# A single-core decoder trunk: the scale row as a one-row product, its load first, filled weight buffers, and a new step list for the pooling mixer

## The chip, the cores and the metric

The kernel runs on 1 core of one Trainium2 chip. The metric is device time in microseconds (us) of one execution. The kernel before takes 899.64 us, the median of 3 runs (898.89 to 899.78 us).

## The reference

The reference is a small transformer trunk over 512 tokens of 1024 channels with two layers. Layer 0 mixes tokens by causal pooling, layer 1 by stick-breaking attention, and each is followed by a squared-ReLU MLP with sandwich RMSNorm. The change touches only the pooling mixer of layer 0:

```
h = rms_norm(x, mix_pre_g[0])
for g, w in enumerate((2, 4, 8, 16)):        # four groups of 256 channels
    y[:, g] = mean of the last w tokens of h[:, g]  -  h[:, g]
    m[:, g] = y[:, g] @ pool_w[g]            # 256 x 256
m = m * pool_scale                           # one factor per channel
x = x + rms_norm(m, mix_post_g[0])
h = rms_norm(x, mlp_pre_g[0])
x = x + rms_norm(square(relu(h @ w_up[0])) @ w_down[0], mlp_post_g[0])
```

## The kernel before

**Tiles.** Tokens lie in four tiles of 128 (`x0` to `x3`, 128 x 1024 fp32, 512 KB each). A fp32 product with one half as two rounded parts (`xnh`, `xnl` against high and low weights) makes the big products of the MLP; the mixer's own products are plain fp32, which TensorE does in two passes each.

**The mixer's stages.** For each token tile: the sum of squares (`q`, halves on ScalarE and VectorE for tiles 0 and 1, whole on ScalarE for 2 and 3), the reciprocal root on GpSimd (`v`), the pooling bands scaled by it (`b`, tile `own`), the pooling as a product of `x` with `own` (`p`, TensorE, line 875), its copy from PSUM to SBUF (`c`, ScalarE), the part that reaches over from the tile before (`f`, VectorE, line 892), the 256 x 256 maps (`m`, TensorE, line 903), squares (`s`, ScalarE, line 316) and product with the post gain (`g`, VectorE, line 368) of the result, its reciprocal root (`V`), the sum into `x` (`a`, VectorE, line 387), squares of `x` (`S`), root (`W`), norm (`n`, line 430), transposes (`t`, TensorE, line 438), and the split of the transposed tile into high (`h`, ScalarE, line 448) and low (`l`, VectorE, line 457). The digits behind a letter are the token tile and the half. Four up products of the MLP follow inside the mixer (`u`, lines 764 to 768; 24 products of 256 columns each, over token tiles 0 and 1); `i` and `k` split their weights (lines 920 and 924).

**The scale.** `pool_scale` and the pre gain are multiplied into the pooling weights (`w`, VectorE, line 832, four pieces of 256 columns for each half). The weights lie channel by partition, so the scale row is spread over 128 partitions by a product with a tile of ones (`r`, line 821): `row` is a 128 x 1024 tile whose first partition holds the row and whose others are filled with zeros on VectorE and GpSimd; `e` copies the result from PSUM.

**What sets the order.** `MIX_ORDER` is the list of these steps. Inside it the program order of TensorE, ScalarE, VectorE and GpSimd is exactly that list, so a step that waits holds every later step of its engine. `z8` is eight products on a zero tile, ahead of everything else on TensorE. SyncE's queue issues the loads in the order in which they are written, and a load that must wait for a buffer holds all loads behind it. The scale row alone is loaded from ScalarE's queue, after the table load of line 134 and both fills.

Of the kernel before, what the change touches and what calls it, by code (L numbers as in the profile page):

```python
# [10 lines left out]
F32 = mybir.dt.float32  # L11
# [4 lines left out]
P = 128  # L16
D = 1024
# [16 lines left out]
NS = [slice(0, 512), slice(512, 1024)]  # L34
# [10 lines left out]
def woven(x, c, n=S):  # L45
# [13 lines left out]

MIX_ORDER = [  # L60
    (w[0], [int(w[1:])] if w[0] == "z" else [int(c) for c in w[1:]])
    for w in """z8 q00 q01 r1 v0 b0 q10 r0 q11 v1 p02 p01 b1 p00 c02 e0 p12 c01 p11 w0 e1 p10 c00 c12 q2 q3 m00 w1 c11 v2 c10
    s00 f11 m01 m11 s01 b2 j0 v3 f10 m10 p22 g00 b3 i0 s11 p20 V0 g01 p21 p32 s10 a01 a00 V1 k0 S00 g10 S01 g11
    p31 c20 c21 p30 c31 c22 a11 f20 a10 W0 m20 n01 n00 S11 f21 g20 S10 t01 c30 c32 f30 W1 s20 t00 n10 f31 h00
    m21 t10 n11 i1 l00 t11 h10 k1 m31 s21 h01 l10 g21 V2 l01 i2 a20 m30 a21 s31 h11 s30 S20 l11 g31 S21 u0 V3 W2
    u1 g30 a31 a30 n21 i3 S31 n20 t21 t20 S30 k2 k3 h20 W3 h21 n30 u2 n31 t30 l20 t31 l21 u3 h30 h31 l30 l31""".split()
]


# [49 lines left out]
R_SCALE, R_MIX_POST0, R_MLP_PRE0, R_MLP_POST0, R_MIX_POST1, R_MLP_POST1 = range(6)  # L119
# [5 lines left out]
def trunk(ctx, tc, x, bands, grow, pw, wup, wdn, wq, wk, wv, wo, out):  # L125
    nc = tc.nc
# [4 lines left out]
    psum = pool("psum", 8, space=bass.MemoryType.PSUM)  # L131
    dram = pool("dram", space=bass.MemoryType.DRAM)

    nc.scalar.preload_act_table_set("sigmoid_and_others")

    uid = [0]

# [24 lines left out]
    def spare_tile():  # L162
        return work.tile([P, D], F32, tag="spare", name=name("spare"))
# [3 lines left out]
    def gain_row(r, t=None):  # L167
        t = work.tile([P, D], F32, tag="grow", name=name("grow")) if t is None else t
        rows.append(nc.sync.dma_start(t, grow[r : r + 1, :].broadcast_to((P, D))))
        return t  # L170
# [603 lines left out]


    with tc.tile_pool(name="mix0", bufs=1, reuse_waits="tile") as mp:
        warm = mp.tile([P, 512], mybir.dt.bfloat16, tag="warm", name="warm")
        nc.gpsimd.memset(warm, 0.0)

# [5 lines left out]
        later = packed[:, :half].bitcast(mybir.dt.bfloat16).rearrange("p (w c) -> p w c", w=NW)  # L785
        first = packed[:, half:].rearrange("p (w c) -> p w c", w=NW)

        row = mp.tile([P, D], F32, tag="row", name="row")
        nc.vector.memset(row[:, NS[0]], 0.0)
        nc.gpsimd.memset(row[:, NS[1]], 0.0)  # L790
        ones = mp.tile([P, P], F32, tag="ones", name="ones")
        nc.gpsimd.memset(ones, 1.0)
        at = D + P + 4 * KC
        wpool = [mp.tile([P, n], F32, tag=f"pw{i}", name=f"pw{i}") for i, n in enumerate((at, D))]
        nc.scalar.dma_start(row[:1], grow[R_SCALE : R_SCALE + 1, :])
        with tc.manual_schedule(engines={mybir.EngineType.SP}):
            nc.sync.dma_start(packed, bands)
            nc.sync.dma_start(xt[1], x[TS[1], :])
            nc.sync.dma_start(wpool[0], pw[:, :at])
            nc.sync.dma_start(xt[2], x[TS[2], :])  # L800
            nc.sync.dma_start(wpool[1], pw[:, at:])
            nc.sync.dma_start(xt[3], x[TS[3], :])
            gpost = gain_row(R_MIX_POST0)
            gpre0 = gain_row(R_MLP_PRE0, spare_tile())
# [613 lines left out]
```

## Time and profile before

| What | us |
|---|---|
| median of 3 runs | 899.64 |
| lowest and highest run | 898.89, 899.78 |
| the profiled execution | 899.84 |
| its span in the profile | 898.1 |
| TensorE (PE) busy | 888.9 (99%) |
| VectorE (DVE) busy | 690.4 (77%) |
| ScalarE (ACT) busy | 555.6 (62%) |
| GpSimd (POOL) busy | 37.8 (4%) |

The profiled execution lies 1.7 us above its span, which is what lies around the span, and 0.2 us above the median. Busy time of an engine is the time in which at least one of its instructions runs. PE's products overlap: one of 256 columns lasts 0.38 us in the records while the next one starts 0.216 us later, so a group's own length is its first start to the next group's first start. PEld is the weight load that goes ahead of a product; DMA landings count from the issue.

### The profile page before, as it was taken

How to read it: one execution, taken by the hardware profiler on the slowest of the kernel's cores; microseconds unless marked ns; L12 is line 12 of the kernel's file. 1: busy time of each engine (PE TensorE's matmuls, PEld its weight loads, DVE VectorE, ACT ScalarE, POOL GpSimd, SP SyncE). 2: the span in 40 equal slices, each digit the busy share in tenths (PEclk: the TensorE clock that was granted, in tenths of full speed). 3: DMA queues.
4: the chain of work that ended last, by engine and by line, in shares of the span. 5: the costliest groups of instructions: out<-in, count | busy, mean ns of one | idle time of the engine just before them, and what ended most of it. 6: DMA issues, size and time to landing. Idle time of an engine off the chain costs nothing.

```text
span 898.1 us, 12323 instructions
## 1 busy us (share of the span) xinstructions
PE 888.9 (99%) x4688; PEld 786.5 (88%) x4688; DVE 690.4 (77%) x800; ACT 555.6 (62%) x984; POOL 37.8 (4%) x78
## 2 busy tenths in 40 slices
PE   9999999999999999999999999999999999999997
PEld 6998888888888888888999888998888888888886
DVE  6876799998988977268777478884696976968866
ACT  6667679898796947256455464875545444444632
POOL 3200000000000004000000000200000000000002
PEclk9999999999999999999999999999999999999999
DMA  8446969889698750643152272442514233133002
GB/s 303 147 148 217 344 233 340 326 277 410 220 342 285 285 189 2 209 166 134 56 187 93 95 281 71 153 176 96 186 40 164 79 140 117 47 141 118 24 1 94
DMA packets 42685, 155.73 MB, mean 173 GB/s; under 512 B 4225, under 2 KB 4353, under 8 KB 42626
## 3 DMA queue, kind: packets, MB, share of 16 engines
q1 hardware_dynamic: 42624, 154.94, 47.9%
q8 instruction: 37, 0.61, 0.3%
q14 instruction: 22, 0.18, 0.1%
q10 hardware_dynamic: 2, 0.00, 0.0%
HBM read 121.38 MB, written 33.55 MB: 173 GB/s over the span
## 4 chain that ended last, share of the span: by engine, by line
PE 87%; DVE 4%; DMA 4%; ACT 3%; issue 2%; POOL 0%; SPq 0%; POOLq 0%; ACTq 0%; DVEq 0%
PE ps L638 24%; PE ps L767 14%; PE ps L764 14%; PE ps L768 14%; PE ps L331 4%; PE ps L333 4%; PE ps L332 4%; DMA xn<-in_wdn 2%; PE ps L1133 2%; PE ps L1114 2%; PE ps L1158 2%; PE ps L903 1%; PE ps L438 1%; DVE w L313 1%; DMA x<-in_x 1%
## 5 line engine op out<-in xcount | busy, mean ns | idle before, releaser
L638 PE MATMUL ps<-w,a 128*128 128x512 f32 x1176 | 266.3, 379 | 0.7 <-ACT a L312 0.7
L767 PE MATMUL ps<-xnh,w 128*128 128x512 f32 (+1 forms) x704 | 253.4, 362 | 0.0
L768 PE MATMUL ps<-xnl,w 128*128 128x512 f32 (+1 forms) x704 | 252.8, 360 | 0.0
L764 PE MATMUL ps<-xnh,w 128*128 128x512 f32 (+1 forms) x704 | 252.2, 360 | 0.3 <-DVE w L924 0.3
L638 PEld LDWEIGHTS ps<-w,a 128*128 128x128 f32 x1176 | 222.0, 189 | 32.9 <-ACT a L312 1.1
L764 PEld LDWEIGHTS ps<-xnh,w 128*128 128x128 f32 x704 | 132.9, 190 | 15.9 <-DVE w L924 0.4
L768 PEld LDWEIGHTS ps<-xnl,w 128*128 128x128 f32 x704 | 133.5, 190 | 15.2
L767 PEld LDWEIGHTS ps<-xnh,w 128*128 128x128 f32 x704 | 133.0, 190 | 15.3
L192 DVE TENSOR_TENSOR w<-raw,w 128x1024 fp32r<-128x1024 f32 x58 | 70.8, 1221 | 48.4 <-ACT w L190 48.4
L190 ACT CAST w<-raw 128x1024 fp32r<-128x1024 f32 x58 | 60.6, 1044 | 69.2 <-PE ps L764 68.2
L647 DVE TENSOR_TENSOR y<-ps,y 128x512 f32<-128x512 f32 x124 | 83.7, 684 | 24.5 <-PE ps L638 24.2
L312 ACT CAST a<-r 128x768 fp32r<-128x768 f32 (+1 forms) x60 | 47.4, 790 | 56.0 <-PE ps L638 36.5
L312 ACT CAST w<-e 128x1536 fp32r<-128x1536 f32 (+1 forms) x30 | 41.8, 1392 | 34.3 <-DVE e L612 26.2
L313 DVE TENSOR_TENSOR a<-r,a 128x768 fp32r<-128x768 f32 (+1 forms) x60 | 53.9, 898 | 8.3 <-ACT a L312 8.3
L1095 DVE TENSOR_TENSOR_SCAN e<-u,begin 128x1280 f32<-128x1280 f32 x16 | 45.2, 2825 | 18.6 <-ACT u L1079 17.9
L313 DVE TENSOR_TENSOR w<-e,w 128x1536 fp32r<-128x1536 f32 (+1 forms) x30 | 49.3, 1644 | 0.7 <-ACT w L312 0.5
L202 ACT ACTIVATE apart<-apart,eye 128x128 f32<-128x128 f32 (+1 forms) x128 | 42.4, 409 | 0.0
L313 DVE TENSOR_TENSOR w<-w,w 128x1536 fp32r<-128x1536 f32 (+1 forms) x20 | 33.0, 1648 | 4.7 <-ACT w L312 4.7
L674 ACT ACTIVATE r<-r 128x512 f32<-128x512 f32 x56 | 35.3, 630 | 1.3
L313 DVE TENSOR_TENSOR w<-xn,w 128x1536 fp32r<-128x1536 f32 (+1 forms) x20 | 33.0, 1649 | 3.7 <-ACT w L312 3.3
L673 ACT ACTIVATE r<-ps 128x512 f32<-128x512 f32 x56 | 33.1, 591 | 3.9 <-PE ps L764 3.9
L312 ACT CAST w<-w 128x1536 fp32r<-128x1536 f32 (+1 forms) x20 | 27.7, 1385 | 5.9 <-DMA w<-in_wdn 5.9
(148 smaller groups left out, 1293.4 us busy)
## 6 DMA issues: line engine op xcount, KB each, us to landing
raw<-in_wup SPq DMA_DIRECT2D x64, 512.0 KB, 3.8
w<-kept SPq DMA_DIRECT2D x60, 512.0 KB, 4.3
kept<-wx SPq DMA_DIRECT2D x30, 512.0 KB, 5.2
kept<-apart SPq DMA_DIRECT2D x24, 512.0 KB, 5.9
w<-in_wdn SPq DMA_DIRECT2D x8, 1536.0 KB, 7.4
xn<-in_wdn SPq DMA_DIRECT2D x8, 1536.0 KB, 8.3
apart<-in_wq SPq DMA_DIRECT2D x7, 512.0 KB, 6.9
kept<-spare SPq DMA_DIRECT2D x6, 512.0 KB, 6.0
```

Source lines behind the costliest of these rows:

```text
L190: nc.scalar.copy(hi, raw)
L192: nc.vector.tensor_tensor(out=lo, in0=raw, in1=hi.bitcast(F32), op=ALU.subtract)
L202: nc.scalar.mul(c, c, gc[:, at : at + 1])
L312: latest["act"] = nc.scalar.copy(hi, src)
L313: latest["dve"] = nc.vector.tensor_tensor(out=lo, in0=src, in1=hi.bitcast(F32), op=ALU.subtract)
L331: nc.tensor.matmul(dst, ah, bh, start=start, stop=False)
L638: nc.tensor.matmul(bank, a[:, x, q, TS[t]], woven(w[:, z, q], NS[0]), start=start and q == 0 and k == 0, stop=q == self.n - 1 and k == 2, ...
L647: nc.vector.tensor_tensor(out=part, in0=bank, in1=part, op=ALU.add)
L764: nc.tensor.matmul(pu[:, cols], wl[:, k, :], moving(xnh, k), start=False, stop=k == KC - 1)
L767: nc.tensor.matmul(pu[:, cols], wh[:, k, :], moving(xnh, k), start=k == 0, stop=False)
L768: nc.tensor.matmul(pu[:, cols], wh[:, k, :], moving(xnl, k), start=False, stop=False)
L1095: nc.vector.tensor_tensor_scan(out=self.e[:, ::-1], data0=self.u[:, 1:][:, ::-1], data1=begin[:, ::-1], initial=0.0, op0=ALU.mult, op1=ALU ...
```

## The change

The zero fills of `row` go, and `row` becomes a single partition; the product that spreads it has one row instead of 128. Its load is the first instruction of ScalarE, ahead of the activation table load. GpSimd fills the first 512 columns of the second weight tile and the 1184 columns of the first with zeros, and the loads of those tiles must wait for the fills. On SyncE's queue the second weight tile goes ahead of `x2`. The step list is written anew, with one zero product fewer.

```
--- before.py
+++ after.py
@@ -59,11 +59,12 @@
 
 MIX_ORDER = [
     (w[0], [int(w[1:])] if w[0] == "z" else [int(c) for c in w[1:]])
-    for w in """z8 q00 q01 r1 v0 b0 q10 r0 q11 v1 p02 p01 b1 p00 c02 e0 p12 c01 p11 w0 e1 p10 c00 c12 q2 q3 m00 w1 c11 v2 c10
-    s00 f11 m01 m11 s01 b2 j0 v3 f10 m10 p22 g00 b3 i0 s11 p20 V0 g01 p21 p32 s10 a01 a00 V1 k0 S00 g10 S01 g11
-    p31 c20 c21 p30 c31 c22 a11 f20 a10 W0 m20 n01 n00 S11 f21 g20 S10 t01 c30 c32 f30 W1 s20 t00 n10 f31 h00
-    m21 t10 n11 i1 l00 t11 h10 k1 m31 s21 h01 l10 g21 V2 l01 i2 a20 m30 a21 s31 h11 s30 S20 l11 g31 S21 u0 V3 W2
-    u1 g30 a31 a30 n21 i3 S31 n20 t21 t20 S30 k2 k3 h20 W3 h21 n30 u2 n31 t30 l20 t31 l21 u3 h30 h31 l30 l31""".split()
+    for w in """z7 q00 q01 r0 r1 v0 b0 q10 q11 v1 p00 p01 b1 p02 e0 c01 e1 c02 p12 w0 c00 c12 w1 p10 p11 c10 c11 m00 f11
+    m01 q2 v2 q3 m11 s00 f10 s01 m10 s11 b2 g00 i0 p21 g01 p20 v3 j0 V0 b3 s10 g11 a00 S00 a01 c21 c20 p22 p31
+    V1 S01 g10 p30 k0 c22 a10 f20 a11 c31 m20 p32 S10 W0 f21 S11 c30 W1 s20 c32 n01 n00 t01 i1 m21 g20 f30 s21
+    n10 t10 f31 t00 n11 t11 g21 k1 h00 V2 h10 h01 l00 a21 h11 a20 m30 l10 l11 l01 m31 u0 S21 S20 s31 W2 i2 s30
+    V3 n20 n21 t21 t20 g31 h20 g30 a31 h21 S31 a30 k2 u1 S30 i3 W3 l20 n30 u2 t30 n31 t31 h31 h30 k3 l21 l31
+    l30 u3""".split()
 ]
 
 
@@ -131,7 +132,6 @@
     psum = pool("psum", 8, space=bass.MemoryType.PSUM)
     dram = pool("dram", space=bass.MemoryType.DRAM)
 
-    nc.scalar.preload_act_table_set("sigmoid_and_others")
 
     uid = [0]
 
@@ -774,6 +774,10 @@
 
 
     with tc.tile_pool(name="mix0", bufs=1, reuse_waits="tile") as mp:
+        row = mp.tile([1, D], F32, tag="row", name="row")
+        with tc.manual_schedule(engines={mybir.EngineType.Activation}):
+            nc.scalar.dma_start(row, grow[R_SCALE : R_SCALE + 1, :])
+            nc.scalar.preload_act_table_set("sigmoid_and_others")
         warm = mp.tile([P, 512], mybir.dt.bfloat16, tag="warm", name="warm")
         nc.gpsimd.memset(warm, 0.0)
 
@@ -785,20 +789,18 @@
         later = packed[:, :half].bitcast(mybir.dt.bfloat16).rearrange("p (w c) -> p w c", w=NW)
         first = packed[:, half:].rearrange("p (w c) -> p w c", w=NW)
 
-        row = mp.tile([P, D], F32, tag="row", name="row")
-        nc.vector.memset(row[:, NS[0]], 0.0)
-        nc.gpsimd.memset(row[:, NS[1]], 0.0)
-        ones = mp.tile([P, P], F32, tag="ones", name="ones")
+        ones = mp.tile([1, P], F32, tag="ones", name="ones")
         nc.gpsimd.memset(ones, 1.0)
         at = D + P + 4 * KC
         wpool = [mp.tile([P, n], F32, tag=f"pw{i}", name=f"pw{i}") for i, n in enumerate((at, D))]
-        nc.scalar.dma_start(row[:1], grow[R_SCALE : R_SCALE + 1, :])
+        nc.gpsimd.memset(wpool[1][:, :512], 0.0)
+        nc.gpsimd.memset(wpool[0], 0.0)
         with tc.manual_schedule(engines={mybir.EngineType.SP}):
             nc.sync.dma_start(packed, bands)
             nc.sync.dma_start(xt[1], x[TS[1], :])
             nc.sync.dma_start(wpool[0], pw[:, :at])
+            nc.sync.dma_start(wpool[1], pw[:, at:])
             nc.sync.dma_start(xt[2], x[TS[2], :])
-            nc.sync.dma_start(wpool[1], pw[:, at:])
             nc.sync.dma_start(xt[3], x[TS[3], :])
             gpost = gain_row(R_MIX_POST0)
             gpre0 = gain_row(R_MLP_PRE0, spare_tile())
```

On TensorE, the pooling of token tiles 2 and 3 (line 875, `own2`, `own3`) and the first map of tile 2 (`ps37` before, `ps36` after, line 903 or 905). Before:

```order
L875 MATMUL ps30_235<-own2_224,x2_72 128x144 x2
L875 MATMUL ps31_243<-own2_224,x2_72 128x144 x3
L875 MATMUL ps32_250<-own2_224,x2_72 128x144 x3
L875 MATMUL ps33_254<-own3_239,x3_73 128x144 x2
L875 MATMUL ps34_267<-own3_239,x3_73 128x144 x3
L875 MATMUL ps35_274<-own3_239,x3_73 128x144 x3
L903 MATMUL ps37_288<-pw0_92,y2_271 128x256 x4
L438 MATMUL ps38_299<-eye_74,xn3_78 128x128 x4
```

The same stretch of TensorE now:

```order
L877 MATMUL ps30_237<-own2_233,x2_71 128x144 x3
L877 MATMUL ps31_242<-own2_233,x2_71 128x144 x3
L877 MATMUL ps32_261<-own2_233,x2_71 128x144 x2
L877 MATMUL ps33_264<-own3_251,x3_72 128x144 x3
L877 MATMUL ps34_272<-own3_251,x3_72 128x144 x3
L905 MATMUL ps36_285<-pw0_94,y2_258 128x256 x4
L877 MATMUL ps37_290<-own3_251,x3_72 128x144 x2
L438 MATMUL ps38_305<-eye_73,xn3_77 128x128 x4
```

The map of tile 2 stands ahead of the last two pooling products of tile 3 instead of behind them.

On VectorE, from the sum into `x0` (line 387) to the reach of tile 2 (line 892 before, 894 after, `y2`), on which that map waits. Before:

```order
L387 SCALAR_TENSOR_TENSOR x0_70<-m0_194,stat24_195,x0_70 128x512 x2
L924 TENSOR_TENSOR w5_113<-raw4_111,w5_113 128x1024
L368 TENSOR_TENSOR m1_216<-ps29_230,grow1_103 128x512
L368 TENSOR_TENSOR m1_216<-ps28_218,grow1_103 128x512
L387 SCALAR_TENSOR_TENSOR x1_71<-m1_216,stat27_217,x1_71 128x512
L892 TENSOR_TENSOR y2_271<-y2_271,y1_186 128x4x16
```

The same stretch of VectorE now:

```order
L368 TENSOR_TENSOR m1_217<-ps28_219,grow1_106 128x512
L387 SCALAR_TENSOR_TENSOR x0_69<-m0_196,stat22_197,x0_69 128x512 x2
L368 TENSOR_TENSOR m1_217<-ps29_227,grow1_106 128x512
L926 TENSOR_TENSOR w5_116<-raw4_114,w5_116 128x1024
L387 SCALAR_TENSOR_TENSOR x1_70<-m1_217,stat27_218,x1_70 128x512
L894 TENSOR_TENSOR y2_258<-y2_258,y1_180 128x4x16
```

A product with the post gain (line 368, `m1`) has moved ahead of the sum into `x0`; it reads a map of tile 1 that TensorE makes late.

On VectorE, the split of the transposed tiles 0 and 1 (line 457, `xnl`) around the sum into `x2` (line 387). The second row of `xnl` before, and likewise after, is the one of tile 1, half 0. Before:

```order
L457 TENSOR_TENSOR xnl_80<-ps39_310,xnh_79 128x4x128
L924 TENSOR_TENSOR w7_116<-raw6_114,w7_116 128x1024
L457 TENSOR_TENSOR xnl_80<-ps41_323,xnh_79 128x4x128
L368 TENSOR_TENSOR m2_286<-ps40_318,grow1_103 128x512
L457 TENSOR_TENSOR xnl_80<-ps38_299,xnh_79 128x4x128
L387 SCALAR_TENSOR_TENSOR x2_72<-m2_286,stat36_287,x2_72 128x512 x2
L457 TENSOR_TENSOR xnl_80<-ps42_331,xnh_79 128x4x128
```

The same stretch of VectorE now:

```order
L368 TENSOR_TENSOR m2_283<-ps39_311,grow1_106 128x512
L926 TENSOR_TENSOR w7_119<-raw6_117,w7_119 128x1024
L457 TENSOR_TENSOR xnl_79<-ps41_326,xnh_78 128x4x128
L387 SCALAR_TENSOR_TENSOR x2_71<-m2_283,stat35_284,x2_71 128x512 x2
L457 TENSOR_TENSOR xnl_79<-ps40_320,xnh_78 128x4x128
L457 TENSOR_TENSOR xnl_79<-ps42_332,xnh_78 128x4x128
L457 TENSOR_TENSOR xnl_79<-ps38_305,xnh_78 128x4x128
```

The product with the post gain of `m2` stands ahead of all four splits, and the sum into `x2` ahead of three of them. Behind the mixer the rows of all engines follow one another as before.

## Rows read from the trace of the kernel before

**Rows 1.** The page's head, and the two short waits of PE in the mixer.
```profile
span 898.1 us, 12323 instructions
...
PE ps L764 <- DVE w L924: 0.3, 1, 0.3
PE ps L875 <- DVE own L863: 0.3, 1, 0.3
```

**Rows 2.** Stretches: start:end, length, busy PE, PEld, DVE, ACT, POOL, PEclk, DMA share, GB/s.
```profile
0.00:5.70 5.70, 4.28 (x9) 1.54 (x10) 1.46 (x5) 2.00 (x3) 1.71 (x8) 1.00 0.69 217
7.70:12.10 4.40, 4.14 (x33) 3.92 (x32) 3.19 (x11) 4.05 (x9) 0.55 (x1) 1.00 1.01 400
0.00:898.10 898.10, 888.92 (x4688) 786.49 (x4688) 690.35 (x800) 555.62 (x984) 37.78 (x78) 1.00 0.48 173
```

**Rows 3.** Timeline of PE in the mixer: start, length, line, out<-in.
```profile
1.30 3.59 PE L816 MATMUL ps<-warm 128*128 128x512 bf16 x8 [1.30 <-POOL warm L778]
5.02 2.85 PE L821 MATMUL ps<-row,ones 128*128 128x512 f32 x4
7.71 2.12 PE L875 MATMUL ps<-own,x 128*128 128x144 f32 x16
10.09 2.23 PE L875 MATMUL ps<-own,x 128*128 128x144 f32 x16 [0.26 <-DVE own L863]
12.15 7.07 PE L903 MATMUL ps<-pw,y 128*128 128x256 f32 x32
19.06 4.08 PE L875 MATMUL ps<-own,x 128*128 128x144 f32 x32
24.70 1.04 PE L438 MATMUL ps<-eye,xn 128*128 128x128 f32 x8
```

**Rows 4.** Timeline of PE's weight loads for the scale row.
```profile
6.00 0.34 PEld L821 LDWEIGHTS ps<-row,ones 128*128 128x128 f32 x1 [0.52 <-issue]
6.85 0.19 PEld L821 LDWEIGHTS ps<-row,ones 128*128 128x128 f32 x1 [0.51 <-issue]
```

**Rows 5.** Loads and fills at the start: issues, a landing (KB, us), GpSimd's fill.
```profile
2.10 0.43 SPq L799 DMA_DIRECT2D pw<-in_pw  x1
...
1.74 0.50 ACTq L795 DMA_DIRECT2D row<-in_grow  x1
...
pw<-in_pw SPq DMA_DIRECT2D x1, 592.0 KB, 7.2
...
1.18 0.53 POOL L790 MEMSET row<- 128x512 f32 x1
```

**Rows 6.** Timeline of ACT: squares of `x1`, then squares of a map.
```profile
7.87 0.63 ACT L316 ACTIVATE junk<-x 128x512 f32<-128x512 f32 x1 [1.25 <-DMA x<-in_x]
...
15.06 0.61 ACT L316 ACTIVATE xn<-ps 128x512 f32<-128x512 f32 x1
15.55 0.21 ACT L316 ACTIVATION_READ_ACCUMULATOR xn<-ps 128x1 f32 x1
```

**Rows 7.** Timeline of DVE: weights scaled, a reach, then splits and sums.
```profile
9.95 1.67 DVE L832 SCALAR_TENSOR_TENSOR pw<-pw,scale 128x256 f32<-128x256 f32 x4
...
22.30 0.21 DVE L892 TENSOR_TENSOR y<-y,y 128x64 f32<-128x64 f32 x1
...
27.77 1.23 DVE L924 TENSOR_TENSOR w<-raw,w 128x1024 fp32r<-128x1024 f32 x1
28.91 0.68 DVE L457 TENSOR_TENSOR xnl<-ps,xnh 128x512 fp32r<-128x512 f32 x1
29.51 0.68 DVE L368 TENSOR_TENSOR m<-ps,grow 128x512 f32<-128x512 f32 x1
30.11 0.68 DVE L457 TENSOR_TENSOR xnl<-ps,xnh 128x512 fp32r<-128x512 f32 x1
30.71 1.41 DVE L387 SCALAR_TENSOR_TENSOR x<-m,stat,x 128x512 f32<-128x512 f32 x2
32.03 0.69 DVE L457 TENSOR_TENSOR xnl<-ps,xnh 128x512 fp32r<-128x512 f32 x1
```

## The prediction, made before the run

> **What bounds the kernel now.** I read the span first, then the table of stretches, then PE's timeline. PE is busy for 888.92 of 898.10 us [rows 2], so at most 9.2 us can come from its waits anywhere, and the change touches only the first 45 us. There PE starts at 1.30, runs zero products, spreads the scale row from 5.02, pools token tile 0 from 7.71, waits 0.26 us for `own1`, pools tile 1 from 10.09, and then goes from 12.15 into the maps and from 19.06 into the pooling of tiles 2 and 3 without a wait [rows 3]. One more wait stands in the mixer, 0.3 us of the up products for a split weight of line 924 [rows 1]. So the reader is to see a PE-bound mixer: a step list or a load that moves other engines' work gains at most these two waits and what leaves PE's own list, and it loses whatever new wait it makes. Behind the mixer the rows of all engines keep their order, so I carry a shift of PE's end of the mixer to the end one for one.
>
> **The change part by part: the start.** One zero product goes. Eight take 3.59 us; with the 0.16 us overlap of the last taken off that is 0.43 each [rows 3], so the scale product starts at 4.59 in place of 5.02. Its length is not changed by the partitions it contracts: two products of 512 columns in two fp32 passes. The passes show TensorE's clock: the second one lasts from 6.00 to 6.85, 0.85 us, the last two together from 6.85 to 7.71, 0.43 each [rows 3, 4]. That is the lower level (1.2 GHz) up to 6.85 and the upper one (2.4 GHz) from there, though the clock column says 1.00 for the whole stretch [rows 2]. If the rise stays at 6.85, moving everything 0.43 earlier leaves the third pass 0.43 us at the lower level (half of it done) and 0.21 at the upper, then the fourth 0.43: end at 7.49 in place of 7.71, a gain of 0.21. If the rise moves with the work the gain is 0.43; if the missing product puts it off, 0. I take 0.21, the case that leaves the rise where the row has it.
>
> The Trainium skill (TensorE: Matmul & The Clock Gate, What's actually happening) says that the activity window runs freely and does not start with the kernel, so the rise varies from run to run. No run here shows that yet; by it this term would spread over 0 to 0.43 between runs, which is inside the spread of the three runs of before.
>
> The row's load leaves ScalarE's queue about 1 us earlier than the 1.74 of before [rows 5]. Before, it had landed by 5.02, at most 3.3 us after its issue; from about 0.75 that gives at the latest 4.0, and it is needed at 4.59. The table load behind it ends about 0.5 us later than before, and ScalarE does nothing until `x0`, so that costs nothing. If the row came after 4.59, each us would cost one.
>
> **`x1` and the wait for `own1`.** GpSimd's fill of 512 columns took 0.53 us [rows 5]; 512 and 1184 columns make 1.76 us at that rate, from about 1.4, so the first weight load is issued at about 3.0 in place of 2.10 [rows 5], and the four loads behind it shift likewise by 0.9. `x0`, the bands and `x1` are 1.23 MB, and by 5.70 us 1.24 MB had moved (217 GB/s over 5.7 us) [rows 2]; still `x1` was only there at 7.87, when ScalarE's 1.25 us wait ended [rows 6]. So about 2.1 us of later loads went between. With those 0.9 us later, I estimate `x1` at 6.9, with bounds of 5.7 (its bytes alone) and 7.9 (nothing gained). From its landing to the pooling of tile 1 it took 7.87 to 10.09, 2.2 us [rows 3, 6]; so `own1` is ready at 9.1. The pooling of tile 0 ends at 7.49 + 2.12 = 9.61 and nothing waits: the 0.26 us go. The decision lies at a landing of 7.4. Start in all: -0.21 - 0.26 = **-0.47**.
>
> The Trainium skill (DMA: Bandwidth & Descriptors, Queues, rings and completion order) has each DMA engine take descriptors of one ring in order, and speaks against this step: loads behind `x1` in SyncE's queue could then not hold it up, and putting them off would bring nothing. The 2.1 us between bytes and landing stand against a strict order, but completion lag would look the same. What this gives is the first rival below.
>
> **What the fills put off.** The first weights landed at 2.10 + 7.2 = 9.3 [rows 5]. They land between 9.3 (the bytes ahead of them are the same) and 10.4. Their scaling takes 1.67 us for four pieces [rows 7], so the first piece is there at 9.8 to 10.9; the first map starts at 11.67 and takes a piece each 0.43 us (7.07 less 0.16, over 32 passes, 0.216 a pass) [rows 3]. The second weights move ahead of `x2`, one load of 512 KB earlier, 1.3 us at the 400 GB/s of that stretch [rows 2], and are scaled by 13.4 at the latest, when their map begins. Both are hidden behind PE's pooling; the cover ends when the first weights land after 11.2, and then each us costs one. `x2` becomes 1.3 us later, at worst 2.2; its bytes end at 2.88 MB, which is 5.70 + 1.64 MB at 400 GB/s = 9.8, with the 2.1 us lag 11.9, at worst 12.8, with 2.2 us and another 0.5 for whole-width squares 15.5. PE reaches it at 18.6: hidden. GpSimd is free by 3.2 and first needed after 5: hidden. The fills of `row` that go lay in idle time: nothing.
>
> **First new wait: the map of tile 2.** It needs the reach `f20` on VectorE. Now the list there is: product `g11`, two sums into `x0`, `g10`, weight split, sum, reach. `g11` starts after map `m11` has ended on PE and ScalarE has squared it (0.16 + 0.70, from 15.06 to 15.76 [rows 6]). From there VectorE needs 0.60 (28.91 to 29.51) + 1.32 (two sums, 30.71 to 32.03) + 0.60 + 1.14 (27.77 to 28.91) + 0.67 + 0.21 [rows 7], with 0.1 for hand-overs: 5.50 us after `m11`. PE fills it with one map, 1.73, and 28 of the 32 pooling passes of 19.06, 3.92 x 28/32 = 3.43 [rows 3]: 5.16. New wait **+0.3**. Before, four more passes (0.49) stood ahead and the sums did not wait for `g11`.
>
> **Second new wait: the first up product.** It needs the low part `l10`. After map `m21` ends: 0.16 + 0.70 squares, 0.60 `g21`, 1.14 weight split, 0.60 `l00`, 1.32 two sums into `x2`, 0.69 `l10` itself [rows 6, 7], 0.1: 5.3 us. PE has three transposes (0.44 each: 1.04 less 0.16, halved) and two maps (1.73 each) [rows 3]: 4.8. The first high product goes ahead (0.11). New wait **+0.4**. Bounds for each: 0, if a hand-over is quicker than I sum, to 0.8, with one more VectorE step in between.
>
> **The old wait on line 924** (0.3 [rows 1]) was the third product of the third up block, held by a split that stood behind two norms. Now the norms of tile 2 go earlier, and from `l10` to that split's end VectorE has two splits, two norms, two products, two sums and the split (1.2 + 1.3 + 1.2 + 1.3 + 1.2 = 6.2 us), against 6.5 on PE (two blocks of 24 at 0.11, two transposes, 0.33). I keep 0.1 of it: **-0.2**, with bounds of -0.3 and +0.5.
>
> **Sum.** -0.47 + 0.3 + 0.4 - 0.2 = +0.03. The profiled execution took 899.84, 0.2 us above the median of the runs, so against the median 899.64 the forecast is 899.7.
>
> **The rivals.** *`x1` is no earlier*: it lands at 7.9, `own1` is ready at 10.09 as before, and the start gains nothing; -0.47 is lost: 900.2. For it: a load in order ahead needs no help. Against it: the 2.1 us lag, which grew only once other loads were under way. *The two new waits do not come*: the step list was only summed by hand, and a few tenths of slack are all that lie between; without them 899.0. *The clock rises later*, slower than before: the rise came 5.55 us after PE's first product (1.30 to 6.85). If the row comes late and opens a gap, or the zero products no longer suffice, it comes 5.55 us after the scale product instead, at 10.1, and PE does 3.3 us at half rate: +1.65, with the new waits and a gap of 0.3 about +2.0: 901.6. It decides against me when the rise lies beyond 10. Against it: only one product of eight is gone. *The fills do not hold the loads at all* changes only the first term, as the first rival does.
>
> **How the numbers follow.** A measurement tells about 0.2% (1.8 us) from no change. Forecast 899.7: 0.60. `x1` no earlier, 900.2: 0.16. No new waits, 899.0: 0.12. Later rise, 901.6 and above: 0.07. Something outside this account, in the 9.2 us of waits elsewhere, either way: 0.05. The first three lie within 0.2%. Slower by more: 0.07 from the rise, 0.03 from the rest and from the upper bounds adding up, 0.10. Faster by more than 1.8 us would need most waits of the mixer and the low-clock passes at once: 0.06. No change: 0.84. The range takes the bounds of the terms (-0.9 to +1.5) and half of the 0.9 us between the runs: 898.3 to 901.6.
>
> **What would show it.** Right: ScalarE's first squares of `x1` before 7.4, no wait of PE on `own1`, the scale product from 4.6 to 7.5, waits of some tenths on `f20` and on `l10`, PE's busy time within 1 us. Wrong: passes of 0.85 us after 7.5, scaled weights after 11.7, or a PE wait of over 1 us in the first 45 us.

## The result, and the profile after

The changed kernel took 902.76 us (median of 21 runs, 898.67 to 905.08), the kernel before 899.25 in runs beside it (21, 897.98 to 901.53): a ratio of 1.0028 with a 95% interval of 1.0017 to 1.0039, slower by 1.5 to 3.5 us. (The ratio is an estimate of its own and not the quotient of the two medians, which are 3.5 us apart.) Forecast were 899.7, within 898.3 to 901.6. The profiled execution took 905.08 us; it is the slowest of the 21, so its excess over that of before (5.24 us) is larger than the typical one.

The page's head and busy times of the changed kernel, which answer to [rows 1] and the last of [rows 2]:

```profile
span 903.1 us, 12318 instructions
...
PE 892.4 (99%) x4687; PEld 790.2 (87%) x4687; DVE 690.2 (76%) x799; ACT 555.9 (62%) x984; POOL 37.8 (4%) x79
```

One matmul record less, and yet PE is busy 3.5 us longer than 888.92: some matmuls have become slower. PE's waits (line, releaser: us in total, times, longest):

```profile
PE ps L638 <- ACT a L312: 2.3, 1, 2.3
PE ps L818 <- POOL warm L782: 1.3, 1, 1.3
PE ps L768 <- DVE xnl L457: 0.3, 1, 0.3
PE ps L905 <- DVE y L894: 0.2, 1, 0.2
```

The waits for `own1` and for the split weight of line 924 [rows 1] are gone, and the two forecast ones have come: the map (line 905) on the reach, the up product (line 768) on `xnl`. The wait at line 638 stands far behind the mixer, and there was one of 0.68 before. Now PE's timeline, beside [rows 3], with two rows of line 638 added:

```profile
1.30 3.17 PE L818 MATMUL ps<-warm 128*128 128x512 bf16 x7 [1.30 <-POOL warm L782]
4.39 3.78 PE L823 MATMUL ps<-row,ones 1*128 1x512 f32 x4
8.10 6.65 PE L877 MATMUL ps<-own,x 128*128 128x144 f32 x32
14.59 7.07 PE L905 MATMUL ps<-pw,y 128*128 128x256 f32 x32
...
25.29 2.00 PE L905 MATMUL ps<-pw,y 128*128 128x256 f32 x8 [0.20 <-DVE y L894]
...
35.22 0.38 PE L768 MATMUL ps<-xnl,w 128*128 128x256 f32 x1 [0.28 <-DVE xnl L457]
...
154.11 3.62 PE L638 MATMUL ps<-w,a 128*128 128x512 f32 x16
...
177.89 1.13 PE L638 MATMUL ps<-w,a 128*128 128x512 f32 x4 [2.33 <-ACT a L312]
```

The same two places of line 638 in the kernel before:

```profile
151.06 3.62 PE L638 MATMUL ps<-w,a 128*128 128x512 f32 x16
...
172.83 1.13 PE L638 MATMUL ps<-w,a 128*128 128x512 f32 x4 [0.68 <-ACT a L312]
```

These rows split the loss at three points. The first maps start at 14.59 in place of 12.15: +2.44. From there to the group of 16 it takes 139.52 in place of 138.91: +0.61. From that group to the wait's end it takes 23.78 in place of 21.77: +2.01. The sum, 5.06, is the longer span (903.1 - 898.1 = 5.0) to within 0.1.

The 2.44 are not waits. The scale product lasts 3.78 where it lasted 2.85, and 32 pooling passes last 6.65 where 16 and 16 lasted 2.12 and 2.23. Its last two weight loads, beside [rows 4]:

```profile
5.41 0.33 PEld L823 LDWEIGHTS ps<-row,ones 1*128 1x128 f32 x1 [0.52 <-issue]
6.26 0.33 PEld L823 LDWEIGHTS ps<-row,ones 1*128 1x128 f32 x1 [0.52 <-issue]
```

Both take 0.33 us, not 0.19, and lie 0.85 apart: TensorE is still at the lower level (1.2 GHz) when the product ends at 8.17; passes of 0.85 us after 7.5 were the first sign that I had named for being wrong. It stays there through most of the pooling, as the table of stretches for line 877 shows (start:end, length, busy PE and PEld with their instructions, PEclk, DMA share, GB/s):

```profile
8.00:9.00 1.00, 0.90 (x4) 0.90 (x5) 1.00 0.99 405
...
11.00:12.00 1.00, 1.00 (x6) 1.00 (x6) 1.00 1.12 356
...
13.00:14.00 1.00, 1.00 (x10) 1.00 (x9) 1.00 1.00 406
```

A pooling pass takes 0.24 us at the lower level and 0.12 at the upper, and the pass in which the length changes puts the rise at 13.2. It was at 6.8 before. The clock column reads 1.00 in all of these rows all the same. The trace file keeps the times at which the clock changed, and its first entry is the rise itself (13.17 here, 6.83 before); the column counts the time ahead of that entry as full. So the level at the start is read from durations, and the two agree.

The rows that answer to [rows 5 to 7]: an issue, GpSimd's fill, ScalarE's squares of `x1`, VectorE's scaling of weights.

```profile
3.00 0.43 SPq L801 DMA_DIRECT2D pw<-in_pw  x1
...
1.79 1.08 POOL L797 MEMSET pw<- 128x1184 f32 x1
...
7.88 0.63 ACT L316 ACTIVATE junk<-x 128x512 f32<-128x512 f32 x1 [0.96 <-DMA x<-in_x]
...
9.96 1.67 DVE L834 SCALAR_TENSOR_TENSOR pw<-pw,scale 128x256 f32<-128x256 f32 x4
...
12.43 1.67 DVE L834 SCALAR_TENSOR_TENSOR pw<-pw,pw,scale 128x256 f32<-128x256 f32 x4 [0.81 <-ACT scale L826]
```

The first weights are issued at 3.00 as forecast and scaled by 11.63, long before the late maps ask for them. But ScalarE's squares of `x1` start at 7.88, against 7.87 before: in this execution the fills have not brought it forward.

### The profile page after: what moved, and what is told of

It reads as the page before. It is cut to its first block, busy times and chain, and to the rows that moved or that the text cites. A ratio compares the mean times of both kernels' runs of the same rounds, so it can differ in the third digit from the quotient of the medians.

```text
span 903.1 us, 12318 instructions
## 1 busy us (share of the span) xinstructions
PE 892.4 (99%) x4687; PEld 790.2 (87%) x4687; DVE 690.2 (76%) x799; ACT 555.9 (62%) x984; POOL 37.8 (4%) x79
## 4 chain that ended last, share of the span: by engine, by line
PE 86%; DVE 6%; DMA 3%; ACT 3%; issue 1%; POOL 0%; POOLq 0%; SPq 0%; ACTq 0%; DVEq 0%
PE ps L638 24%; PE ps L767 14%; PE ps L768 14%; PE ps L764 14%; PE ps L331 4%; PE ps L333 4%; PE ps L332 4%; PE ps L1135 2%; PE ps L1116 2%; PE ps L1160 2%; DMA kept<-wx 2%; DMA xn<-in_wdn 1%; PE ps L905 1%; PE ps L438 1%; PE ps L877 1%
## 5 line engine op out<-in xcount | busy, mean ns | idle before, releaser
L320 POOL TENSOR_SCALAR stat<-stat,eps 128x1 f32<-128x1 f32 x8 | 5.4, 679 | 604.6 <-ACT xn L316 604.6
```

## The experiments

The question is why the clock rises late. Theory A: the product that contracts one row does not count for the clock as one that contracts 128 does, so after the zero products TensorE is kept at the lower level until the pooling has run a while. Theory B, the prediction's own later-rise rival: the zero product taken away is what was missing. Theory C: the new list, the fills and the loads do it. Ratios are to runs of the kernel before made beside each kernel; the last column counts the runs of more than 901 us. It points to a late rise only where the start is otherwise alike; e1, e6 and e9 have a gap or a longer warm-up besides.

| kernel | median us (low to high, runs) | ratio [95%] | over 901 us |
|---|---|---|---|
| after, from above | 902.76 (898.67 to 905.08, 21) | 1.0028 [1.0017, 1.0039] | 15 of 21 |
| before, beside e1 to e4 | 899.13 | | 2 of 35 |
| e1_full_row | 901.69 (899.64 to 906.21, 12) | 1.0030 [1.0015, 1.0044] | 9 of 12 |
| e2_one_row | 900.61 (897.67 to 903.84, 12) | 1.0014 [1.0001, 1.0027] | 6 of 12 |
| e3_z8 | 902.39 (899.74 to 903.45, 12) | 1.0028 [1.0019, 1.0037] | 8 of 12 |
| e4_before_z7 | 898.89 (897.96 to 899.81, 11) | 0.9994 [0.9985, 1.0002] | 0 of 11 |
| before, beside e5 to e8 | 899.54 | | 3 of 35 |
| e5_full_row_split | 899.75 (898.75 to 902.91, 12) | 1.0008 [0.9996, 1.0020] | 2 of 12 |
| e6_z15 | 901.31 (900.35 to 905.86, 11) | 1.0026 [1.0014, 1.0038] | 8 of 11 |
| e7_before_new_list | 900.17 (899.03 to 902.41, 12) | 1.0005 [0.9994, 1.0016] | 2 of 12 |
| e8_old_list | 902.06 (897.86 to 905.79, 12) | 1.0023 [1.0009, 1.0038] | 9 of 12 |
| before, beside e9 and e10 | 899.30 | | 1 of 19 |
| e9_row_late | 901.46 (900.48 to 905.71, 8) | 1.0030 [1.0012, 1.0048] | 6 of 8 |
| e10_half_rows | 901.43 (899.05 to 903.60, 12) | 1.0023 [1.0011, 1.0034] | 8 of 12 |

The profiled execution of each kernel, with the rise as the trace file has it; the lengths of the passes agree (us):

| kernel | clock rises | first maps start | time of that execution |
|---|---|---|---|
| before | 6.8 | 12.15 | 899.84 |
| after | 13.2 | 14.59 | 905.08 |
| e11_look (after again) | 13.4 | 14.69 | 903.97 |
| e12_look (after again) | 5.0 | 11.21 | 899.65 |
| e1_full_row | 9.6 | 13.57 | 905.85 |
| e2_one_row | 5.2 | 11.15 | 897.97 |
| e3_z8 | 13.4 | 14.92 | 902.68 |
| e4_before_z7 | 5.7 | 10.98 | 897.98 |
| e5_full_row_split | 5.9 | 10.89 | 898.78 |
| e6_z15 | 5.2 | 12.50 | 900.35 |
| e7_before_new_list | 10.75 | 13.57 | 902.41 |
| e8_old_list | 13.2 | 14.84 | 902.70 |
| e9_row_late | 5.8 | 12.88 | 900.48 |
| e10_half_rows | 10.6 | 13.39 | 901.86 |

Take the start of the maps and the wait at line 638 (told of below) off each of these times, and nearly the same is left everywhere: 886.8 to 887.1 in the four kernels with the old list (before, e2, e4, e8), 887.6 to 888.2 in the others, and 889.3 in e1. So these executions differ by the start of the maps, by that wait, and by about 0.9 us for the list; e1 has a loss of its own.

**Full rows again, filled by VectorE (e1).**

```diff
-        row = mp.tile([1, D], F32, tag="row", name="row")
+        row = mp.tile([P, D], F32, tag="row", name="row")
+        nc.vector.memset(row, 0.0)
...
-            nc.scalar.dma_start(row, grow[R_SCALE : R_SCALE + 1, :])
+            nc.scalar.dma_start(row[:1], grow[R_SCALE : R_SCALE + 1, :])
...
-        ones = mp.tile([1, P], F32, tag="ones", name="ones")
+        ones = mp.tile([P, P], F32, tag="ones", name="ones")
```

> The changed kernel, but its scale product contracts 128 partitions again (zeros under the row, ones 128 x 128); all else as changed. Theory A (TensorE's clock rises late, at 13.3 in place of 6.85 us in the profiles, because a product of one row does not count as work for the clock): the rise comes back to about 7, PE's pooling passes take 0.13 us, the time falls to 899.5 (898.5 to 900.5). Theory B (the missing eighth zero product delays the rise): the rise stays near 13, 902.8. Theory C (the new list and the moved loads make the mixer slow): 902.8, with pooling passes that are slow or waiting.

Measured: 901.69, a miss for A as it stood, with a cause of its own. The row came late, and PE stood still between the zero products and the scale product. The fill of 1024 columns ahead of the load moved its issue to 1.98 only, from 1.74 before; that execution's landing was late besides, 4.1 us after the issue:

```profile
6.15 3.66 PE L824 MATMUL ps<-row,ones 128*128 128x512 f32 x4 [1.69 <-DMA row<-in_grow]
```

The rise came at 9.6. The run changed two things at once, the rows and the gap, and tells nothing between A and B; e5 repeats it without the gap.

**The kernel before, with one row (e2).**

```diff
-        row = mp.tile([P, D], F32, tag="row", name="row")
-        nc.vector.memset(row[:, NS[0]], 0.0)
-        nc.gpsimd.memset(row[:, NS[1]], 0.0)
-        ones = mp.tile([P, P], F32, tag="ones", name="ones")
+        row = mp.tile([1, D], F32, tag="row", name="row")
+        ones = mp.tile([1, P], F32, tag="ones", name="ones")
```

> The kernel before with one edit: row and ones have one partition, no zero fills. Theory A: the rise comes at 10 to 13.5 us, pooling passes at half rate, 902.3 (901 to 904). Theories B and C: 899.3, as before.

Measured: 900.61, slower with an interval just above 1. That is under the 901 to 904 of A and above the 899.3 of B and C. The runs lie on two sides: six of 12 below 900, six above 901, and none between. The profiled one is of the lower side (897.97) and rose early, so no trace of this kernel shows a late rise; the six runs above 901 fit one. Of the kernel before, two of 35 runs beside it lie above 901. By the times, one row can do it without the new list and the fills, but not in each execution.

**The change with eight zero products (e3), the kernel before with seven (e4).** One word of the list each; shown for e3, while e4 turns `z8` into `z7` in the list of before:

```diff
-    for w in """z7 q00 q01 r0 r1 v0 b0 q10 q11 v1 p00 p01 b1 p02 e0 c01 e1 c02 p12 w0 c00 c12 w1 p10 p11 c10 c11 m00 f11
+    for w in """z8 q00 q01 r0 r1 v0 b0 q10 q11 v1 p00 p01 b1 p02 e0 c01 e1 c02 p12 w0 c00 c12 w1 p10 p11 c10 c11 m00 f11
```

> The changed kernel with eight zero products in place of seven. Theory A: still late, 902.8 (901.5 to 904). Theory B: the rise returns to about 7, 899.5. Theory C: 902.8 or 0.4 more.

> The kernel before with seven zero products in place of eight, nothing else. Theory A: 899.1 (898.5 to 900), since the full product still counts. Theory B: 902.5. Theory C: 899.1.

Measured: 902.39 and 898.89. The eighth product back makes nothing better, and without it the kernel before is no slower. B falls from both sides. In the trace of e4 the scale product of full rows starts after a wait of 0.25 and reaches the upper level at 5.7:

```profile
4.71 2.44 PE L821 MATMUL ps<-row,ones 128*128 128x512 f32 x4 [0.25 <-DMA row<-in_grow]
6.99 4.15 PE L875 MATMUL ps<-own,x 128*128 128x144 f32 x32
10.98 7.17 PE L903 MATMUL ps<-pw,y 128*128 128x256 f32 x32
```

**Full rows again, without the gap (e5).** The fill is halved between VectorE and GpSimd, and the row is loaded behind the table, as before the change; list, fills of the weights and loads stay those of the change.

```diff
-        row = mp.tile([1, D], F32, tag="row", name="row")
-        with tc.manual_schedule(engines={mybir.EngineType.Activation}):
-            nc.scalar.dma_start(row, grow[R_SCALE : R_SCALE + 1, :])
-            nc.scalar.preload_act_table_set("sigmoid_and_others")
+        row = mp.tile([P, D], F32, tag="row", name="row")
+        nc.vector.memset(row[:, NS[0]], 0.0)
...
+        nc.gpsimd.memset(row[:, NS[1]], 0.0)
+        with tc.manual_schedule(engines={mybir.EngineType.Activation}):
+            nc.scalar.preload_act_table_set("sigmoid_and_others")
+            nc.scalar.dma_start(row[:1], grow[R_SCALE : R_SCALE + 1, :])
...
+        ones = mp.tile([P, P], F32, tag="ones", name="ones")
```

> The changed kernel with the product over 128 partitions and the row's fills, table load and row load where the kernel before has them (half on VectorE, half on GpSimd), so that no gap opens on PE ahead of it; list, filled weights and load order as changed. Theory A (a product of one row does not hold the clock's activity up, so TensorE stays at half rate for some us more in most executions): the rise comes at 5 to 7.5 us, 899.3 + 0.5 for the two short waits of the new list = 899.8 (899.2 to 900.6), runs within 3 us of one another. Theory C (the new list, the fills or the load order hold the mixer up by themselves): 902 to 903.

Measured: 899.75, not to be told from before, and 3.0 under the changed kernel's median. With the list, the fills of the weights and the new order of their loads in place, the full product with its fills and its later row load brings the rise back to 5.9, as A says, and C falls for those three. Three things went back at once, though; e10 takes the rows apart from the other two.

```profile
4.52 2.61 PE L825 MATMUL ps<-row,ones 128*128 128x512 f32 x4
6.97 4.08 PE L879 MATMUL ps<-own,x 128*128 128x144 f32 x32
10.89 7.07 PE L907 MATMUL ps<-pw,y 128*128 128x256 f32 x32
```

**Half of the rows (e10).** Against e5:

```diff
-        row = mp.tile([P, D], F32, tag="row", name="row")
+        row = mp.tile([P // 2, D], F32, tag="row", name="row")
...
-        ones = mp.tile([P, P], F32, tag="ones", name="ones")
+        ones = mp.tile([P // 2, P], F32, tag="ones", name="ones")
```

> The kernel of the run on the full product with its fills split between the engines, but the product contracts 64 partitions. Theory A in its strict form (only the share of the array counts, a full product is needed): 901 to 902.5, runs 5 to 6 us apart. Theory A in a weak form (one row is too few, half is enough): 899.8, as with 128 partitions.

Measured: 901.43, within the strict form's 901 to 902.5. The scale product of 64 rows stays at the lower level to its end (3.75 us, like one row in the change and unlike 128 in e5), and the rise comes at 10.6:

```profile
4.54 3.75 PE L825 MATMUL ps<-row,ones 64*128 64x512 f32 x4
```

The zero fill and the order of the row's load are those of e5, so neither makes the difference between these two; the number of rows contracted is what is left. That rests on one profiled execution of each and on 12 runs of each, whose intervals overlap (from 1.0011 for e10, up to 1.0020 for e5).

**Fifteen zero products ahead of one row (e6).** In the list of the change:

```diff
-    for w in """z7 q00 q01 r0 r1 v0 b0 q10 q11 v1 p00 p01 b1 p02 e0 c01 e1 c02 p12 w0 c00 c12 w1 p10 p11 c10 c11 m00 f11
+    for w in """z15 q00 q01 r0 r1 v0 b0 q10 q11 v1 p00 p01 b1 p02 e0 c01 e1 c02 p12 w0 c00 c12 w1 p10 p11 c10 c11 m00 f11
```

> The changed kernel with fifteen zero products in place of seven, which keep PE at full products to about 7 us; then the one-row product, 1.7 us at full rate, and the pooling from about 9 in place of 8.1. Theory A: the rise comes during the zero products (5 to 7.5 us); mixer about 1.5 us shorter than the changed kernel in the profile although PE does 8 products more; 900.8 (900 to 901.8), and runs closer together. Theory C: 903.5 or more.

Measured: 901.31, half a microsecond above A's 900.8, which lies at the interval's lower end. The rise is at 5.2, under the zero products, and the one-row product behind it takes 1.98 us, all at the upper level:

```profile
1.30 5.33 PE L818 MATMUL ps<-warm 128*128 128x512 bf16 x15 [1.30 <-POOL warm L782]
6.57 1.98 PE L823 MATMUL ps<-row,ones 1*128 1x512 f32 x4
```

But the zero products themselves last 5.33, and the maps start at 12.50: 2.1 us before those of the changed kernel (14.59) and 1.3 behind those of its early execution (11.21, e12). Ten of the 11 runs lie within 900.35 to 901.98, closer together as A said, and one at 905.86.

**The new list alone (e7), and all but it (e8).** e7 is the kernel before with the change's list; e8 the changed kernel with the list of before, so their diffs are the list alone.

> The kernel before with the new step list alone (seven zero products, row of 128 partitions, no fills of the weights, loads in the old order). Theory A: 899.3 + 0.5 = 899.8 (899 to 900.6), the two waits of 0.2 to 0.4 us stand on PE. Theory C with the list as cause: 902.5.

> The changed kernel with the old step list (eight zero products): one-row product, row load first, filled weights, new load order stay. Theory A: like the one-row product alone (900.6, range of 6 us) or up to 1 us more. Theory C with the list as cause: 899.3; with fills or load order as cause: 902 to 903.

Measured: 900.17 (0.63 above before, not to be told from it) and 902.06. With full rows and the new list (e7) the loss is gone, with one row and the old list (e8) it stays; C falls for the list. e8 lies 0.5 above what A allowed and where C put fills or load order as the cause. e5 has the fills and the new order of the weights and takes 899.75, so those are out. The row's load ahead of the table load is not: e8, e3 and the changed kernel have it and lie above 901 in most runs, e2 has one row without it and does so in half. No kernel has full rows, that load and no gap; 6 of 12 and 9 of 12 (e2, e8) do not tell the two apart. e7's own profiled execution had its rise at 10.75, behind a row load that left a gap of 0.56 us, and took 902.41:

```profile
5.03 3.75 PE L822 MATMUL ps<-row,ones 128*128 128x512 f32 x4 [0.56 <-DMA row<-in_grow]
```

**The scale product behind the pooling (e9).** 13 zero products, then the pooling of tiles 0 and 1, the one-row product between them:

```diff
-    for w in """z7 q00 q01 r0 r1 v0 b0 q10 q11 v1 p00 p01 b1 p02 e0 c01 e1 c02 p12 w0 c00 c12 w1 p10 p11 c10 c11 m00 f11
+    for w in """z13 q00 q01 v0 b0 q10 q11 v1 p00 p01 b1 p02 r0 r1 c01 c00 e0 c02 e1 p12 w0 c12 w1 p10 p11 c10 c11 m00 f11
```

> The changed kernel with thirteen zero products, and the one-row product moved behind the pooling of token tile 0, so that PE does full products without a break from 1.3 to about 8.8 us and the one-row product comes after that, at full rate, 1.7 us. Theory A (one-row products do not count as work for the clock; full ones, of zeros too, do): the rise comes at 5 to 7.5 us and stays; maps start at about 12.5 (14.6 in the changed kernel's profile); 900.3 (899.5 to 901.3). If it is the one row anywhere ahead of the maps that costs (theory D: its operands, its load): 902.8 or more.

The profiled execution:

```profile
6.75 2.23 PE L877 MATMUL ps<-own,x 128*128 128x144 f32 x16 [0.28 <-ACT own L871]
8.91 1.98 PE L823 MATMUL ps<-row,ones 1*128 1x512 f32 x4
10.82 2.23 PE L877 MATMUL ps<-own,x 128*128 128x144 f32 x16
12.88 7.07 PE L905 MATMUL ps<-pw,y 128*128 128x256 f32 x32
```

The clock behaves as A says: up at 5.8, and one row between full products does not bring it down (1.98 us, all at the upper level). The time misses, 901.46 against 900.3 (at most 901.3): the product and the longer warm-up stand on PE's path all the same, and PE waits 0.28 for its bands. This execution took 900.48, the least of the eight; what the others lose besides is not shown.

**The changed kernel again, twice (e11, e12).** No edit, the source is that of the change: two more executions, to see whether the late rise and the time go together in one kernel.

> The changed kernel once more, unedited, to see rise and time in one execution. Theory A: a rise near 13 us goes with 901.5 to 905, a rise below 8 us with 898.5 to 900.5; nothing between but waits of line 638.

> As the look before it: the changed kernel, unedited; theory A ties a rise near 13 us to 901.5 to 905 and a rise below 8 us to 898.5 to 900.5.

```profile
4.39 3.78 PE L823 MATMUL ps<-row,ones 1*128 1x512 f32 x4
8.10 6.75 PE L877 MATMUL ps<-own,x 128*128 128x144 f32 x32
14.69 7.07 PE L905 MATMUL ps<-pw,y 128*128 128x256 f32 x32
```

That was e11 (903.97 us); now e12 (899.65 us):

```profile
4.39 2.25 PE L823 MATMUL ps<-row,ones 1*128 1x512 f32 x4
6.82 4.55 PE L877 MATMUL ps<-own,x 128*128 128x144 f32 x32 [0.18 <-ACT own L871]
11.21 7.07 PE L905 MATMUL ps<-pw,y 128*128 128x256 f32 x32
```

The same instructions, the same start at 4.39: where the clock rises at 5.0, inside the first one-row pass, the kernel is as fast as before; where it rises at 13.4 the maps start 3.48 later and the execution takes 4.32 longer. The other 0.84 are the wait at line 638, 1.49 and 0.66 long. The late rise in two of three profiled executions, 15 of 21 runs over 901 us and a median 3 us above e5 say that it is this kernel's usual course.

## Why the prediction was wrong

**The step that failed** is the first: "Its length is not changed by the partitions it contracts", and after it "I take 0.21, the case that leaves the rise where the row has it". At one level it is so: at the lower one 3.78 us with 1 row (the change), 3.75 with 64 (e10) and 3.75 with 128 (e7). But the partitions decide how soon the level rises, and with it the length of everything up to the maps. The term was -0.21 and measured about +3: that is how far e5's median lies under the changed kernel's, and e11 and e12 give 3.5 for an execution that has the late rise against one that has not. In the start itself there was a gain that I had not counted: the product began at 4.39 and not at 4.59. With eight zero products and the row's load first it begins at 4.83 (e3), so of the 5.02 before about 0.2 us was, as far as that shows, a wait for the row.

**The later-rise rival** had the mechanism and not the trigger. It blamed a gap or the missing zero product, and its "Against it: only one product of eight is gone" weighed the wrong edit; the one row stood in the same diff. It also priced the rise at 10.1 and 1.65 us, where it came at 13.2 to 13.4 and cost 2.4 against the rise of before at 6.8, about 3.5 against one at 5.0. Its other trigger, a gap ahead of the scale product, is borne out in part: e1 (1.69 us) and e7 (0.56 us) rose at 9.6 and 10.75 with full rows, e4 (0.25 us) at 5.7.

**The range.** Its terms' own bounds add up to -1.0 and +2.1, not to the -0.9 and +1.5 that I took. Summed right, the range would have ended at 902.2, and 902.76 lies outside that too.

**The spread of the rise.** I gave it 0 to 0.43 us between runs. The rise lay at 5.0 and at 13.4 in executions of one kernel. The Trainium skill (TensorE: Matmul & The Clock Gate, What's actually happening) says that the point varies with where the first matmul falls in a free-running window, and gives ±500 ns. That it varies by itself agrees; the size does not for this kernel, and there the measurement decides.

**`x1`.** Forecast at 6.9 because of the fills, and 7.88 came. But e11 and e12 are the same kernel, and there `x1` was in use by 6.73 and 6.93; the row of e12:

```profile
6.93 0.63 ACT L316 ACTIVATE junk<-x 128x512 f32<-128x512 f32 x1 [0.16 <-DMA x<-in_x]
```

Of the ten profiled executions with the fills, ScalarE's squares of `x1` start by 7.22 in nine, and the 7.88 is the tenth; without the fills they start at 7.87 and 8.00 in two (before, e7) and at 6.87 and 6.70 in two (e2, e4). So the landing varies by more than 1 us by itself, and these few can't tell whether the fills help it; neither the forecast's 6.9 nor "`x1` no earlier" is shown. In the profiled execution the 0.26 us on `own1` went although `x1` came late, because PE came late enough.

**The step list.** The new waits came where I put them, at 0.20 and 0.28 for +0.3 and +0.4. Each also costs the 0.16 us by which one group of matmuls otherwise overlaps the end of the last, so 0.36 and 0.44 in all, and the old wait of 0.3 left with its own 0.16. That makes +0.34; the rows of before and after show +0.61 net, for the forecast +0.3 + 0.4 - 0.2 = +0.5, and the 0.27 between I can't place. The same 139.5 us from the maps to line 638 stand in e3, e6, e9, e11 and e12. Over the whole execution the list costs about 0.9, by the sums under the second table. The term holds to within 0.4 us, and e7's median agrees with it (+0.63, within its error).

**Hidden parts.** Weights, `x2` and GpSimd were hidden, as forecast: no wait of PE names them but the 1.30 us at the very start, which was there before.

**What I did not have** is the wait at line 638: 0.68 before, 2.33 in the profiled execution of after, 1.49 and 0.66 in e11 and e12, 0.72, 0.84 and 0.38 in e7, e8 and e10, 3.00 in e1, none in e2 to e6 and e9. It does not follow the edits, nor the rise (e3 rose at 13.4 and had none). It explains 2 of the 5.2 us between the profiled executions and little that can be shown between the medians. Followed back from its end, the chain runs over ScalarE and VectorE to the end of a DMA transfer: at 163.33 before (`xn`), 9.5 us ahead of the wait's end, and at 161.24 after (`kept`), 16.6 us ahead of it. What makes that chain longer or shorter stays open. In the wait of e1 the clock fell again, at 176.84, and the four passes behind it were slow, 2.08 us where after has 1.13; that is the loss that e1 has for itself:

```profile
177.18 2.08 PE L638 MATMUL ps<-w,a 128*128 128x512 f32 x4 [3.00 <-ACT a L312]
```

Open too is why a kernel with one row rises early in some executions, and why e2 lies above 901 in half of its runs, where e8 and the changed kernel do so in most.

No version beat the kernel before: the best, e4, cannot be told from it.

## What to carry to other kernels

A product on the way to TensorE's first real work is not free because it is small: here one that contracts a single row left the clock low through some 20 of the next 32 passes, in four of six profiled executions, while zeros in all 128 rows cost nothing that the times show. When an edit touches what runs before the clock has risen, weigh every instruction there by how many rows it contracts, and take both levels into the range. Read the level from durations of like instructions, and compare several executions before an early stretch is called typical.

## What the runs showed of the hardware

- Before the first rise the profile's clock column reads 1.00, in stretches in which passes take 0.24 us in place of 0.12, and 0.85 in place of 0.43. A fall inside the kernel does show: the column reads 0.50 from 176.84 on in e1, in and behind a wait of 3.00 us. The wait of 2.33 us in after brought no fall.
- The rise depends on the rows contracted ahead of it: behind seven or eight zero products, 1 row, up at 13.2 to 13.4 in four profiled executions of six (5.0 and 5.2 in the others, inside the first one-row pass); 64 rows, 10.6 in one; 128 rows behind a gap of at most 0.25 us, 5.7 to 6.8 in three. Full products of zeros alone bring it up (5.2 in e6). Once up, one row does not bring it down (e9).
- A load of 4 KB from ScalarE's queue, issued at 1.73 to 1.98 while the token tiles are moving, could be read by the weight load that waited for it after 2.9 us (4.68, e4), 3.3 (5.00, e7) and 4.1 (6.12, e1).
